# Down projections of a two-layer trunk: seven products of Strassen's scheme for eight, with the sums on GpSimd

## The chip, the cores and the metric

The kernel runs on one core of a Trainium2 chip. The metric is device time in microseconds (us) of one execution; three runs of the kernel before gave 1199.43, 1199.52 and 1201.88 us, median 1199.52. The granted TensorE clock of the profiled execution is 1.000.

## The reference

Two layers of a streaming encoder over 512 tokens of width 1024. Each layer mixes tokens (layer 0 with differential attention, layer 1 with chunked gated linear attention, both beside a cross-attention into 256 memory tokens) and then runs a gated feed-forward network with a causal depthwise convolution of width 3:

```python
def conv_ffn(h, w_up, conv_w, conv_b, w_down):
    u = h @ w_up                                  # 1024 -> 2 x 2816
    c = conv(u, conv_w) + conv_b                  # depthwise, causal, width 3
    a, g = jnp.split(c, 2, axis=-1)
    return (jax.nn.silu(g) * a) @ w_down          # 2816 -> 1024

for i in range(2):
    x = x + concat([mix, cross]) @ w_out[i]
    x = x + conv_ffn(rms_norm(x, ffn_norm[i]), w_up[i], conv_w[i], conv_b[i], w_down[i])
```

The change concerns the last product, `@ w_down`, in both layers: 2816 x 1024 weights against 512 tokens.

## The kernel before

Activations are held transposed, features on the 128 partitions and tokens along the columns: the residual stream is eight tiles `xT[n]` of [128 x 512]. Every large product runs in three TensorE passes on split numbers: a value is kept as a rounded high part (ScalarE copy, line 201 for weights) and the rest as a low part (VectorE subtraction, line 204), and `product` (lines 272 to 274) accumulates high x high, high x low and low x high. Weights come from one packed tensor in blocks of up to 1024 columns: a DMA into a `raw` buffer (three of them), then the split into `whi` and `wlo` (five of each). `weights(key)` hands out the pieces in the order of the list `_pieces` and has the next piece made ahead.

The feed-forward network (`ffn`, from line 1011) has 22 k tiles of 128 hidden features. For each, two up products of 24 matmuls (value half and gate half) go to one of the PSUM banks `ps_mm` and `ps_sm`; VectorE scales the bank into `u` (line 1026), ScalarE and VectorE run the convolution (1028 to 1030), ScalarE the Silu, VectorE the gating product (1057), and the result is split into a pair `mids` (1059 and 1060). After 12 k tiles, and again after the other 10 (`HALVES`), a down stage follows: for four blocks of 256 output features, two banks (`ps_lg`, `ps_tp`) take `product` over the tiles collected so far, each matmul with a [128 x 128] weight tile and 512 tokens, and `update` adds a finished bank to `xT[n]` (line 978). In the last down stage of layer 0 `update` also makes the next layer's operands: high part with the layer's gain (238), low part (239), square (338), running sum of squares (340). In the last stage of layer 1 each tile is sent out.

TensorE's order is as written in the code (a manual schedule over the whole kernel); the other engines are ordered by the scheduler, in the kernel before also beside the down stages. PSUM has eight banks, two for each of the tags `mm`, `sm`, `lg` and `tp`. Layer 1 begins with the projection `gm` of 272 columns (`gemm`, lines 255 to 257), whose first block needs all eight `xh`, `xl` tiles, followed by `token_rsqrt` (346).

Of the kernel before, what the change touches and what calls it, by code (L numbers as in the profile page):

```python
# [21 lines left out]
S = 512  # L22
# [8 lines left out]
HALVES = (6, 5)  # L31
XS = 36
WB = 5
STEPS, FILL = (8, 14, 20, 26), (3.2, 2.5, 1.2, 0.8, 1.3)
# [5 lines left out]
         [(c, (3, 4, 5)) for c in (0, 1, 2)] + [(3, (6, 7, 3, 4, 5))]])  # L40


def _pieces():
# [6 lines left out]
    for l in range(2):  # L50
# [29 lines left out]
def _blocks():  # L80

    out = []
    for key, name, i, ks, ranges in _pieces():
        w = sum(b - a for a, b in ranges)
        step = WTILE // w
        out.append([(name, i, ks[j:j + step], ranges, w) for j in range(0, len(ks), step)])
    return out
# [42 lines left out]
def trunk(ctx, tc, head_d, x_t, mem_t, wpack, cols_a_d, cols_d, conv_d, gate_d, rel_bias, diff_lambda, consts, onehot, out):  # L130
# [75 lines left out]
    def raw_tile():  # L206
        return wp.tile([128, WTILE], F32, name="raw", tag="raw", bufs=3)
# [5 lines left out]

    def make_piece(raws=None, between=None):
        parts = []
# [12 lines left out]
    def weights(key):  # L228
# [748 lines left out]
    def update(n, p, gain, acc):  # L977
        V.tensor_add(xT[n], xT[n], p)
        if gain is None:
            return  # L980
# [30 lines left out]
    def ffn(pool, l, acc):  # L1011
        rB = pool.tile([128, S], F32, name="rB", bufs=1)
        us = [pool.tile([128, S + 2], F32, name=f"u{i}", bufs=1) for i in range(4)]
# [4 lines left out]
        def up(parts, n):  # L1018
# [3 lines left out]
            product(p, parts, n, list(zip(xh, xl)))  # L1022
# [19 lines left out]
        base = 0  # L1042
        for half, nq in enumerate(HALVES):
            mids = []
            for q in range(base, base + nq):
                wa = weights(("ua", l, q))
                wg = None
                for n in range(2):
                    ua = up(wa, n)
                    wg = wg or weights(("ug", l, q))  # L1050
                    if q == 0 and n == 0:
                        row_scales(acc[0])
                    ug = up(wg, n)
                    ca = conv(*ua, 2 * q + n)
                    cg = conv(*ug, 22 + 2 * q + n)
# [112 lines left out]
```

## Time and profile before

| | |
|---|---|
| median of three runs | 1199.52 us |
| span of the profiled execution, first to last instruction | 1195.9 us |
| four down stages | 66.6, 55.6, 66.5 and 55.6 us |
| TensorE matmuls busy | 1178.8 us, 5656 instructions |
| VectorE busy | 761.1 us |
| ScalarE busy | 548.3 us |
| GpSimd busy | 4.5 us, 25 instructions |

The profiled execution's time is known as its span; the whole time that the runs state holds some 3.6 us more than it. In a row of the profile stand the line, the engine, the operation, the written and read tiles with their shapes and the count; then busy time and mean duration, and the idle time of the engine before these instructions with what ended it. PE is TensorE, PEld its weight loads, DVE VectorE, ACT ScalarE, POOL GpSimd, SP the engine that issues most DMAs. Durations of matmuls overlap; starts tell their rate.

### The profile page before, as it was taken

Reading aid. Unit: us, or ns where it says so; the run is one execution under the profiler, and the core shown is the slowest. Engines: PE = TensorE matmul, PEld = TensorE weight load, DVE = VectorE, ACT = ScalarE, POOL = GpSimd, SP = SyncE. Lnnn points to the kernel's source line nnn. Section 1 sums busy time; section 2 is a strip of 40 time slices with the busy share of each in tenths; the row PEclk is TensorE's granted clock in tenths of the full one; section 3 lists DMA queues with packets and bytes.
Section 4 is the critical chain, followed back from the end, with each engine's and each line's share of the span. In section 5 each row is a group of like instructions: output and inputs, shape, how many; then the busy total and the mean of one; then the engine's idle time right before and its main releaser. Section 6 shows DMA issues by size and latency. Waiting matters only on the chain.

```text
span 1195.9 us, 14770 instructions
## 1 busy us (share of the span) xinstructions
PE 1178.8 (99%) x5656; PEld 964.5 (81%) x5656; DVE 761.1 (64%) x1270; ACT 548.3 (46%) x966; POOL 4.5 (0%) x25
## 2 busy tenths in 40 slices
PE   9999998999999999999999999999999999999998
PEld 6887776788888888888888788988888888888887
DVE  7566676777777434767557736768777743476741
ACT  6666676554444322434436534536544422243420
POOL 0000000000000000000000000000000000000000
PEclk9999999999999999999999999999999999999999
DMA  8432213132332332422342221233233233232231
GB/s 296 124 96 80 80 54 119 50 120 92 106 106 71 123 100 63 123 85 89 115 129 93 72 71 58 89 104 125 84 106 105 74 121 106 70 123 72 89 115 44
DMA packets 39268, 117.81 MB, mean 99 GB/s; under 512 B 4671, under 2 KB 6520, under 8 KB 39198
## 3 DMA queue, kind: packets, MB, share of 16 engines
q1 hardware_dynamic: 39054, 116.62, 30.7%
q8 instruction: 44, 0.72, 0.2%
q14 instruction: 26, 0.21, 0.1%
q10 hardware_dynamic: 144, 0.26, 0.1%
HBM read 112.65 MB, written 4.21 MB: 98 GB/s over the span
## 4 chain that ended last, share of the span: by engine, by line
PE 90%; ACT 4%; DVE 3%; DMA 2%; issue 1%; SPq 0%; ACTq 0%; DVEq 0%
PE ps_mm L273 8%; PE ps_mm L274 8%; PE ps_mm L272 8%; PE ps_sm L273 7%; PE ps_sm L272 7%; PE ps_sm L274 7%; PE ps_mm L255 5%; PE ps_mm L257 5%; PE ps_mm L256 5%; PE ps_lg L273 3%; PE ps_lg L272 3%; PE ps_lg L274 3%; PE ps_tp L272 3%; PE ps_tp L273 3%; PE ps_tp L274 3%; PE ps_tp L170 2%
## 5 line engine op out<-in xcount | busy, mean ns | idle before, releaser
L201 ACT CAST whi<-raw 128x1024 fp32r<-128x1024 f32 (+4 forms) x212 | 208.4, 985 | 264.7 <-PE ps_tp L273 134.7
L204 DVE TENSOR_TENSOR wlo<-raw,whi 128x1024 fp32r<-128x1024 f32 (+4 forms) x212 | 241.3, 1140 | 113.3 <-ACT whi L201 110.9
L272 PE MATMUL ps_mm<-xsh,whi 128*128 128x512 f32 x438 | 173.3, 396 | 0.0
L273 PE MATMUL ps_mm<-xsl,whi 128*128 128x512 f32 x438 | 170.6, 390 | 0.2 <-DVE xsl L239 0.2
L274 PE MATMUL ps_mm<-xsh,wlo 128*128 128x512 f32 x438 | 170.6, 390 | 0.0
L272 PE MATMUL ps_sm<-xsh,whi 128*128 128x512 f32 x378 | 147.1, 389 | 0.0
L274 PE MATMUL ps_sm<-xsh,wlo 128*128 128x512 f32 x378 | 147.1, 389 | 0.0
L273 PE MATMUL ps_sm<-xsl,whi 128*128 128x512 f32 x378 | 147.0, 389 | 0.0
L255 PE MATMUL ps_mm<-whi,xsh 128*128 128x512 f32 (+2 forms) x352 | 136.7, 388 | 0.1
L257 PE MATMUL ps_mm<-whi,xsl 128*128 128x512 f32 (+2 forms) x352 | 131.1, 372 | 0.3 <-DVE xsl L239 0.3
L256 PE MATMUL ps_mm<-wlo,xsh 128*128 128x512 f32 (+2 forms) x352 | 130.6, 371 | 0.0
L1028 ACT ACTIVATE cvo<-u,cv 128x512 f32<-128x512 f32 x88 | 71.6, 814 | 121.5 <-DVE u L1026 121.5
L273 PEld LDWEIGHTS ps_mm<-xsl,whi 128*128 128x128 f32 x438 | 82.3, 188 | 17.4 <-DVE xsl L239 0.6
L274 PEld LDWEIGHTS ps_mm<-xsh,wlo 128*128 128x128 f32 x438 | 82.2, 188 | 17.2
L272 PEld LDWEIGHTS ps_mm<-xsh,whi 128*128 128x128 f32 x438 | 82.3, 188 | 17.1 <-issue 0.7
L1029 DVE SCALAR_TENSOR_TENSOR cvo<-u,cv,cvo 128x512 f32<-128x512 f32 x88 | 65.8, 749 | 38.7 <-ACT cvo L1028 38.7
L274 PEld LDWEIGHTS ps_sm<-xsh,wlo 128*128 128x128 f32 x378 | 70.9, 188 | 14.8
L272 PEld LDWEIGHTS ps_sm<-xsh,whi 128*128 128x128 f32 x378 | 71.0, 188 | 14.8
L273 PEld LDWEIGHTS ps_sm<-xsl,whi 128*128 128x128 f32 x378 | 71.0, 188 | 14.6
L255 PEld LDWEIGHTS ps_mm<-whi,xsh 128*128 128x128 f32 x352 | 66.3, 188 | 13.6 <-issue 3.3
L257 PEld LDWEIGHTS ps_mm<-whi,xsl 128*128 128x128 f32 x352 | 66.1, 188 | 12.5 <-DVE xsl L239 0.5
L256 PEld LDWEIGHTS ps_mm<-wlo,xsh 128*128 128x128 f32 x352 | 66.4, 189 | 9.8
(273 smaller groups left out, 1760.6 us busy)
## 6 DMA issues: line engine op xcount, KB each, us to landing
raw<-in_wpack_dram SPq DMA_DIRECT2D x178, 512.0 KB, 3.5
xt<-in_x_t_dram SPq DMA_DIRECT2D x15, 256.0 KB, 6.0
raw<-in_wpack_dram SPq DMA_DIRECT2D x15, 256.0 KB, 2.6
raw<-in_wpack_dram SPq DMA_DIRECT2D x8, 384.0 KB, 3.1
xres<-xt SPq DMA_DIRECT2D x8, 256.0 KB, 2.0
xt<-xres SPq DMA_DIRECT2D x8, 256.0 KB, 3.3
out_dram<-xt SPq DMA_DIRECT2D x8, 256.0 KB, 2.0
bt<-bias_d SPq DMA_DIRECT2D x6, 256.0 KB, 3.6
```

The lines of the kernel that those rows point to most:

```text
L170: nc.tensor.transpose(dst, src, ident[:n, :n])
L201: ins = A.copy(hi[:, c], raw[:, c])
L204: V.tensor_sub(lo[:, c], raw[:, c], hi[:, c].bitcast(F32))
L255: mm(p, sh[k][:, blk(b)], hi, start=k == 0, stop=False)
L256: mm(p, sh[k][:, blk(b)], lo, start=False, stop=False)
L257: mm(p, sl[k][:, blk(b)], hi, start=False, stop=k == KT - 1)
L272: mm(p, hi[:, blk(n)], bh, start=i == first, stop=False)
L273: mm(p, hi[:, blk(n)], bl, start=False, stop=False)
L274: mm(p, lo[:, blk(n)], bh, start=False, stop=i == last)
L1028: A.activation(c, u[:, 2:], AF.Identity, scale=cv[l][:, 2, j:j + 1], bias=cv[l][:, 3, j:j + 1])
L1029: V.scalar_tensor_tensor(c, u[:, 1:S + 1], cv[l][:, 1, j:j + 1], c, op0=ALU.mult, op1=ALU.add)
```

## The change

The down projection of a group of k tiles is cut in two along k (even and odd k tiles of a pair), along the output features (two blocks of 256 within each output half of 512) and along the tokens (two blocks of 256), and is computed with seven products of half size in each direction instead of eight (the variant of Strassen's scheme with 15 additions). The 22 k tiles make 11 pairs, in groups of 3, 4 and 4 pairs (`GROUPS`); after each group a down stage follows, and after the first two groups one further up tile is computed ahead of it. A stage has two output halves of seven products each, in the hand-written order of `DOWN`.

- Weights: per group and output half four quarters are loaded (`a11`, `a12`, `a22` and one that becomes `s3`), GpSimd makes the sums `s1` to `s4` from them, and seven blocks are split by ScalarE and VectorE, where four were. There are six `raw` buffers instead of three, and pieces are made further ahead (`prefetch`).
- Operands: per pair GpSimd makes four [128 x 256] differences (`middle`), and seven operands are split.
- Products: matmuls of a [128 x 128] weight tile with 256 tokens; some products accumulate onto a bank whose earlier state VectorE has already added.
- Additions: each product's state is added from PSUM to quarters of `xT` (`add`), 84 additions of 256 columns per layer.
- In the last group of a layer the first three products run over all pairs but the last one first.
- VectorE, ScalarE and GpSimd keep the written order in the down stages.
- The `us` buffers become slices of one tile at multiples of 544 columns. The scratch size for dynamic DMAs is set to 1024.

```diff
-HALVES = (6, 5)
+GROUPS = (3, 4, 4)
 XS = 36
 WB = 5
+RAWS = 6
+DOWN = ((0, "a11"), (0, "s1"), (0, "a12"), (0, "s2"), (0, "s4"), (0, "s3"), (1, "a11"), (0, "a22"),
+        (1, "s1"), (1, "s2"), (1, "a12"), (1, "s3"), (1, "s4"), (1, "a22"))
...
+def _ffn():
+
+    steps, q = [], 0
+    for i, nq in enumerate(GROUPS):
+        steps += [("up", t) for t in range(2 * q + (i > 0), 2 * (q + nq) + (i + 1 < len(GROUPS)))]
+        steps.append(("down", i))
+        q += nq
+    return steps
...
-        for nq in HALVES:
-            for q in range(base, base + nq):
-                piece(("ua", l, q), "w_up", l, K8, (256 * q, 256 * q + 256))
-                piece(("ug", l, q), "w_up", l, K8, (DFF + 256 * q, DFF + 256 * q + 256))
-            for c in range(4):
-                piece(("dn", l, base, c), "w_down", l, tuple(range(2 * base, 2 * base + 2 * nq)),
-                      (256 * c, 256 * c + 256))
-            base += nq
+        for what, i in _ffn():
+            if what == "up":
+                for h in range(2):
+                    f = DFF * h + 128 * i
+                    piece(("u", l, i, h), "w_up", l, K8, (f, f + 128))
+            else:
+                for c, name in DOWN:
+                    piece(("d", l, i, c, name), "w_down", l, (), (512 * c, 512 * c + 512))
...
+    wsums = {}
+
+    def make_sum(key, todo):
+        n, name = 256 * GROUPS[key[2]], key[4]
+        r = wsums.setdefault(key[:4], {})
+        v = lambda t: r[t][:, :n]
+        if name == "a11":
+            for t in ("a11", "s3", "a22", "a12"):
+                r[t] = load_raw(raw_tile(), n)
+            r["s1"], r["s2"] = raw_tile(), raw_tile()
+            G.tensor_add(v("s1"), v("s3"), v("a22"))
+            G.tensor_sub(v("s2"), v("s1"), v("a11"))
+            G.tensor_sub(v("s3"), v("a11"), v("s3"))
+        if name == "s4":
+            r["s4"] = r["a12"]
+            G.tensor_sub(v("s4"), v("s4"), v("s2"))
+        hi, lo = (wp.tile([128, WTILE], F32R, name=t, tag=t, bufs=WB) for t in ("whi", "wlo"))
+        split_weights(slice(0, n), r[name], hi, lo)
+        return hi, lo
+
     def make_piece(raws=None, between=None):
+        key = plan[len(made)][0]
+        if key[0] == "d":
+            made.append(make_sum(key, blocks[len(made)]))
+            return
...
+    def prefetch(i):
+        size = lambda j: 1 if plan[j][0][0] == "d" else len(blocks[j])
+        by_block = plan[i][0][0] in "ud"
+        while len(made) <= i or (len(made) < len(plan) and (
+                sum(map(size, range(i, len(made) + 1))) <= WB if by_block else len(made) < i + 2)):
+            make_piece()
+
+    def weights(key, more=True):
         i = used[0]
         assert plan[i][0] == key, (plan[i][0], key)
-        while len(made) < min(i + 2, len(plan)):
-            make_piece()
+        if more:
+            prefetch(i)
...
+        if gain is not None:
+            settle(n, gain, acc)
+
+    def settle(n, gain, acc):
         xh[n], xl[n] = split_tiles()
         split(xh[n], xl[n], xT[n], gain(n))
...
+        us = pool.tile([128, 4 * (S + 32)], F32, name="us", bufs=1)
+        us = [us[:, blk(i, S + 32)][:, :S + 2] for i in range(4)]
...
+        def middle(n, m, op, prev):
+            lo, hi = m[:, blk(0, 256)], m[:, blk(1, 256)]
+
+            def put(dst, src):
+                A.copy(dst[:, :, 0:256], src)
+                V.tensor_sub(dst[:, :, 256:512], src, dst[:, :, 0:256].bitcast(F32))
+            one = lambda t: t.rearrange("p (a b) -> p a b", a=1)
+            if n == 0:
+                t = pool.tile([128, 4, 256], F32, name="mt", bufs=1)
+                b11, t1 = (xs.tile([128, S], F32R, name=x, tag="xs", bufs=XS) for x in ("b11", "t1"))
+                G.tensor_sub(t[:, 0], hi, lo)
+                put(one(b11), one(lo))
+                put(one(t1), t[:, 0:1])
+                op.update(b11=b11, t1=t1)
+                return t, hi
+            t, hi0 = prev
+            G.tensor_sub(t[:, 1], hi, t[:, 0])
+            G.tensor_sub(t[:, 2], hi, hi0)
+            G.tensor_sub(t[:, 3], lo, t[:, 1])
+            r = pool.tile([128, 5, S], F32R, name="mid", bufs=max(GROUPS))
+            put(r[:, 0:2], m.rearrange("p (a b) -> p a b", a=2))
+            put(r[:, 2:5], t[:, 1:4])
+            op.update(zip(("b21", "b22", "t2", "t3", "t4"), (r[:, i] for i in range(5))))
+
+        def down(g, mids, finish):
+            last, ks = len(mids) - 1, tuple(range(len(mids)))
+            parts, banks, first = {}, {}, used[0]
+
+            def step(c, tag, w, m, ks=ks, start=False, more=True):
+                if (c, w) not in parts:
+                    parts[c, w] = weights(("d", l, g, c, w), more)
+                elif more:
+                    prefetch(first + more)
+                if start:
+                    banks[c, tag] = bank(tag)
+                p = banks[c, tag]
+                hi, lo = parts[c, w]
+                for k in ks:
+                    mv = mids[k][m]
+                    for n in range(2):
+                        o, ws = p[:, blk(n, 256)], slice(256 * k + 128 * n, 256 * k + 128 * n + 128)
+                        terms = (hi, mv[:, 0:256]), (hi, mv[:, 256:512]), (lo, mv[:, 0:256])
+                        for i, (a, b) in enumerate(terms):
+                            mm(o, a[:, ws], b, start=start and (k, n, i) == (0, 0, 0), stop=k == last and i == 2,
+                               skip_group_check=True)
+
+            def add(c, tag, f, t):
                 for n in range(2):
...
+                    x = xT[4 * c + 2 * f + n][:, blk(t, 256)]
+                    V.tensor_add(x, x, banks[c, tag][:, blk(n, 256)])
+
+            def done(c, f):
                 for n in range(2):
...
+                    finish(4 * c + 2 * f + n)
+            if g + 1 < len(GROUPS):
+                step(0, "lg", "a11", "b11", start=True)
+                add(0, "lg", 0, 0)
+                step(0, "tp", "s1", "t1", start=True)
+                add(0, "tp", 1, 1)
+                step(0, "mm", "a12", "b21", start=True)
+                add(0, "mm", 0, 0)
+            else:
+                step(0, "lg", "a11", "b11", ks[:-1], True)
+                step(0, "tp", "s1", "t1", ks[:-1], True, False)
+                step(0, "mm", "a12", "b21", ks[:-1], True, False)
+                step(0, "lg", "a11", "b11", ks[-1:], more=False)
+                add(0, "lg", 0, 0)
+                step(0, "tp", "s1", "t1", ks[-1:], more=1)
+                add(0, "tp", 1, 1)
+                step(0, "mm", "a12", "b21", ks[-1:], more=2)
+                add(0, "mm", 0, 0)
+            step(0, "lg", "s2", "t2")
+            add(0, "lg", 0, 1)
+            step(0, "tp", "s4", "b22")
+            add(0, "tp", 0, 1)
+            done(0, 0)
+            step(0, "lg", "s3", "t3")
+            add(0, "lg", 1, 1)
+            step(1, "lg", "a11", "b11", start=True)
+            add(1, "lg", 0, 0)
+            step(0, "lg", "a22", "t4")
+            add(0, "lg", 1, 0)
+            done(0, 1)
+            step(1, "tp", "s1", "t1", start=True)
+            add(1, "tp", 1, 1)
+            step(1, "lg", "s2", "t2")
+            add(1, "lg", 0, 1)
+            step(1, "mm", "a12", "b21", start=True)
+            add(1, "mm", 0, 0)
+            step(1, "lg", "s3", "t3")
+            add(1, "lg", 1, 1)
+            step(1, "tp", "s4", "b22")
+            add(1, "tp", 0, 1)
+            done(1, 0)
+            step(1, "lg", "a22", "t4")
+            add(1, "lg", 1, 0)
+            done(1, 1)
+
+        acc2, mids, live = [None], [], []
+
+        def finish(n):
+            if l == 0:
+                settle(n, lambda k: c_attn(1, k), acc2)
+                nc.sync.dma_start(xres[n], xT[n])
+            else:
+                nc.sync.dma_start(out[n], xT[n])
+        for what, i in _ffn():
+            if what == "up":
+                ua = up(weights(("u", l, i, 0)))
+                if i == 0:
+                    row_scales(acc[0])
+                ug = up(weights(("u", l, i, 1)))
+                ca = conv(*ua, i)
+                cg = conv(*ug, 22 + i)
+                A.activation(cg, cg, AF.Silu)
+                V.tensor_mul(ca, ca, cg)
+                if i % 2 == 0:
+                    live = [{}, None]
+                    mids.append(live[0])
+                live[1] = middle(i % 2, ca, *live)
+            else:
+                n, last = GROUPS[i], i == len(GROUPS) - 1
+                if last and l == 0:
+                    tables("natural_log_exp_and_others")
+                with tc.manual_schedule(engines={E.Activation, E.DVE, E.Pool}):
+                    down(i, mids[:n], finish if last else lambda n: None)
+                mids = mids[n:]
         return acc2
```

More of the change, by code (lines that the diff above doesn't have):

```diff
@@ L84, in _blocks @@
         w = sum(b - a for a, b in ranges)
+        if key[0] == "d":
+            base, (f, _) = sum(GROUPS[:key[2]]), ranges[0]
+            ks = [tuple(2 * q + j for q in range(base, base + GROUPS[key[2]])) for j in range(2)]
+            out.append([(name, i, ks[j], ((f + 256 * h, f + 256 * h + 256),), 256)
+                        for h, j in ((0, 0), (1, 0), (1, 1), (0, 1))] if key[4] == "a11" else [])
+            continue
         step = WTILE // w
@@ L206, in raw_tile @@
     def raw_tile():
-        return wp.tile([128, WTILE], F32, name="raw", tag="raw", bufs=3)
+        return wp.tile([128, WTILE], F32, name="raw", tag="raw", bufs=RAWS)
     def load_raw(raw, n):
@@ L1021, in up @@
             p = bank("mm" if i % 4 < 2 else "sm")
[L1022 removed]
+            product(p, parts, 0, list(zip(xh, xl)))
             return p, us[i % 4]
```

43 lines of the change are left out of this document (3 added, 40 removed).

## The prediction

> **What bounds the kernel now.** I read the page first, then the busy time by stage, then the timeline of TensorE and of VectorE where stages meet.
>
> ```profile
> span 1195.9 us, 14770 instructions
> PE 1178.8 (99%) x5656; PEld 964.5 (81%) x5656; DVE 761.1 (64%) x1270; ACT 548.3 (46%) x966; POOL 4.5 (0%) x25
> ...
> PEclk9999999999999999999999999999999999999999
> ...
> PE 90%; ACT 4%; DVE 3%; DMA 2%; issue 1%; SPq 0%; ACTq 0%; DVEq 0%
> ```
>
> TensorE is busy in 99% of the span at the full granted clock, and it makes 90% of the chain that ended last; GpSimd does next to nothing. So fewer TensorE microseconds are worth their whole length, as long as the other engines keep feeding it. Stage by stage (the four down stages, and one up stage):
>
> ```profile
> core 0: us, PE busy (x) PEld busy (x) DVE busy (x) ACT busy (x) POOL busy (x), PEclk, DMA share, GB/s
> ...
> 393.90:460.50 66.60, 66.60 (x290) 54.08 (x290) 23.12 (x25) 14.64 (x16) 0.00 (x0) 1.00 0.31 95
> 460.50:569.30 108.80, 108.80 (x481) 90.07 (x480) 76.31 (x96) 45.44 (x57) 0.00 (x0) 1.00 0.29 92
> 569.30:624.90 55.60, 55.59 (x241) 44.97 (x240) 27.59 (x37) 22.54 (x30) 1.67 (x4) 1.00 0.40 128
> ...
> 961.00:1027.50 66.50, 66.50 (x289) 54.02 (x288) 23.11 (x25) 14.57 (x15) 0.00 (x0) 1.00 0.30 95
> ...
> 1136.40:1192.00 55.60, 55.58 (x241) 44.77 (x239) 16.16 (x20) 9.09 (x11) 0.00 (x0) 1.00 0.24 80
> ```
>
> The down stages take 66.6 + 55.6 + 66.5 + 55.6 = 244.3 us for 2 x (288 + 240) = 1056 matmuls of 512 columns, 231 ns from one to the next; an up stage takes 108.8/480 = 227 ns. In a down stage VectorE works only 23.1 of 66.6 us, in an up stage already 76.3 of 108.8 (70%).
>
> **The products.** The change replaces 8 quarter products by 7, but halves the moving operand: 11 pairs of k tiles x 7 products x 2 output halves x 2 row blocks x 3 terms x 2 layers = 1848 matmuls of 256 columns, each with its own weight load. Does a 256-column matmul cost half? The listed durations overlap, so I read starts in the one place that has this shape in a row, 25 matmuls of the gated layer's last projection:
>
> ```profile
> start us, us, engine line op out<-in xcount [idle before <-releaser]
> 769.46 0.28 PE L257 MATMUL ps_mm<-whi,xsl 128*128 128x256 f32 x1
> ...
> 772.34 0.28 PE L257 MATMUL ps_mm<-whi,xsl 128*128 128x256 f32 x1
> ```
>
> (772.34 - 769.46)/24 = 120 ns, more than half of 227: some 13 ns per matmul don't shrink with the columns. New down time 1848 x 0.120 = 221.8 us, a gain of **22.5 us** (9% of the stage, not the eighth that seven for eight suggests). Bounds: half of 227 would give 209.8 (gain 34.5); if the new tiles cost 7 ns more, as the down stages' 231 against 227 warns at half width and beyond, 127 ns give 234.7 (gain 9.6). I take 120, since it is this very shape with a fresh weight load each time.
>
> **What the other engines must do for it.**
>
> ```profile
> L204 DVE TENSOR_TENSOR wlo<-raw,whi 128x1024 fp32r<-128x1024 f32 x178 | 217.3, 1223 | 92.7 <-ACT whi L201 91.6 <-PE ps_tp L170 0.2
> L201 ACT CAST whi<-raw 128x1024 fp32r<-128x1024 f32 x178 | 187.0, 1052 | 218.7 <-PE ps_tp L273 110.7 <-PE ps_sm L273 61.7 <-issue 25.2
> ...
> L338 ACT ACTIVATE xt<-xt 128x512 f32<-128x512 f32 x35 | 21.4, 621 | 0.0
> L340 DVE TENSOR_TENSOR xt<-xt 128x512 f32<-128x512 f32 x31 | 21.2, 684 | 0.2
> ...
> L978 DVE TENSOR_TENSOR xt<-xt,ps_lg 128x512 f32<-128x512 f32 x16 | 11.0, 688 | 68.4 <-PE ps_lg L274 68.4
> ...
> L204 DVE TENSOR_TENSOR wlo<-raw,whi 128x768 fp32r<-128x768 f32 x8 | 7.6, 956 | 4.6 <-ACT whi L201 3.3 <-DMA xt<-in_x_t_dram 1.3
> ...
> L201 ACT CAST whi<-raw 128x768 fp32r<-128x768 f32 x8 | 6.6, 836 | 9.9 <-PE ps_mm L273 6.3 <-PE ps_mm L257 3.6
> ...
> L204 DVE TENSOR_TENSOR wlo<-raw,whi 128x256 fp32r<-128x256 f32 x8 | 3.4, 420 | 3.9 <-ACT whi L201 3.9
> ...
> L239 DVE SCALAR_TENSOR_TENSOR xsl<-xt,cols_a,xsh 128x512 fp32r<-128x512 f32 x8 | 6.0, 748 | 3.2 <-ACT xsh L238 3.2
> L238 ACT ACTIVATE xsh<-xt,cols_a 128x512 fp32r<-128x512 f32 x8 | 5.8, 726 | 18.2 <-DVE xt L978 18.2
> ...
> L828 POOL MEMSET xt<- 128x512 f32 x1 | 0.5, 530 | 51.8 <-PE ps_tp L170 51.8
> ...
> L435 POOL MEMSET gw<- 96x384 f32 x1 | 0.4, 414 | 0.0
> ...
> raw<-in_wpack_dram SPq DMA_DIRECT2D x178, 512.0 KB, 3.5
> ```
>
> Weight splits in the down stages grow from 22 to 38.5 blocks of 1024 columns per layer (seven summed quarters for four): +16.5 x 1.22 = 20 us on VectorE and 17 on ScalarE. Adds from PSUM go from 16 of 512 columns (11 us) to 84 of 256 at 0.42 (35 us), operand splits from 22 x 0.69 = 15 to 11 x 2.5 = 27 us. That is some 57 us more per layer on VectorE, 64% to about 74% of the span: no new bound. In a group of four pairs one product is 24 x 0.120 = 2.88 us of TensorE, and VectorE has per product one split and two adds, 1.22 + 0.84 = 2.06; in a group of three, 2.16 against 0.96 + 0.84 = 1.80. It keeps up, with little over. The order is written out by hand there: the split for the product four ahead stands in front of this product's adds, and an accumulation into a used bank waits for the add before it. Behind every late sum or split stand adds, and behind these TensorE, with about one product of slack.
>
> The weight loads are as many bytes as before. The reuse of the six raw buffers lets the second half's third tile (3.5 us) land before the first product starts; only the second and later sums of that half wait, for the split of the quarter a22. That is four to five products ahead of use, so I cost the loads at nothing.
>
> GpSimd sums are not in the trace. From below a [128 x 1024] sum can hardly beat VectorE's 1.22 us; from above, three passes (two reads, one write) at the memset's slope, (530 - 414)/128 = 0.9 ns a column, make 2.8 us. I take 2.0, between them: 33 blocks' worth per layer, 66 us beside some 340 us of feed-forward network. [...]
>
> **Where TensorE will wait nonetheless.** First, the last group of each layer, where nothing covers the chain behind the last up product:
>
> ```profile
> 569.50 0.69 DVE L1026 TENSOR_TENSOR u<-ps_sm,rB 128x512 f32<-128x512 f32 x1 [0.59 <-PE ps_sm L274]
> ...
> 573.78 0.69 DVE L1057 TENSOR_TENSOR cvo<-cvo 128x512 f32<-128x512 f32 x1 [0.70 <-ACT cvo L1056]
> ```
>
> The gated product is ready at 574.5, 5.2 us after the last up matmul (569.3). Then come three dependent GpSimd subtractions (some 0.5 us each), a 768-column copy (0.84) and its subtraction (0.96): 8.7 us with the hops, and only behind that VectorE adds the first product (0.84). TensorE has three products to do meanwhile, 8.64 us, and then needs that add: about 1.2 us late, 2.4 in both layers. Second, in layer 0's last group the operands of layer 1 are made between the adds (per tile a scaled copy of 0.73, a square of 0.62 and two VectorE steps). Behind the fifth product's add, which ends 1.0 us after its product, ScalarE has two such tiles, 2.7, and the next split's copy, 1.05; then VectorE has that split's 1.22 and the sixth product's add, 0.84. That is 6.8 us where two products, 5.76, are covered: 1.0 late, the same again behind the eighth product, and I add 1.0 for the shift of the first point: 3 us. Third, the layer boundary:
>
> ```profile
> 624.94 0.29 PE L255 MATMUL ps_mm<-whi,xsh 128*128 128x272 f32 x1
> ...
> 628.30 0.39 PE L257 MATMUL ps_mm<-whi,xsl 128*128 128x272 f32 x1 [0.31 <-DVE xsl L239]
> 628.90 1.05 PE L346 MATMUL ps_sm<-C,xt 128*128 128x1 f32 x8 [0.21 <-DVE xt L340]
> 629.81 0.38 PE L255 MATMUL ps_mm<-whi,xsh 128*128 128x272 f32 x1
> ```
>
> The first 24 matmuls of layer 1 take 4.9 us before, some 1.7 more than fed ones. Now both last tiles get their last add only after the last product. VectorE is then still some 3 us behind with the pair before (adds, two splits, two tiles); the adds take 0.84, and copy, square, copy and low part of the two tiles 0.73 + 0.62 + 0.73 + 0.75 = 2.8: the last operand comes about 7 us after the last product, where the fed matmuls cover 3. Some 4.4 us lost for 1.7: 3 us more than before. Fourth, VectorE's convolutions beside the groups of three: 1 us each, 2. Fifth, two 256-column adds instead of one of 512 at the end: 0.2. Together 10.6 us.
>
> Sixth, GpSimd against VectorE. No row of before shows a two-input sum on GpSimd beside VectorE. From below nothing; from above VectorE stands still during the sums (rival below). I take 2.4 us, 0.4 per group, half a collision of one sum less the slack. [...]
>
> Sum: -22.5 + 10.6 + 2.4 = -9.5. The span is 1195.9 and the median 1199.52, 3.6 us around it, which I leave as they are: **1190.0 us**.
>
> **Rivals.**
> (a) *All fed.* If the queue orders hide the waits, 1199.5 - 22.5 = 1177. For it: VectorE's 2.06 in 2.88. Against it: the chain of 8.7 us is there. Chance 0.15.
> (b) *The shared port decides: slower.* In each group the second half's sums s2, s3, s4 stand back to back on GpSimd, 3 x 2.0 = 6.0 us. If VectorE's splits can't run beside them, the add of the sixth product is 6.0 late against a slack of 2.88 - 1.0 = 1.9: 4.1 us in each of six groups, 24.6. 1199.5 - 22.5 + 10.6 + 24.6 = 1212. [...] It decides from (22.5 - 10.6)/6 = 2.0 us per group. Chance 0.22. About that point, within 0.2% (2.4 us, about what a measurement here can tell from no change): 0.08.
> (c) *Narrow matmuls are dearer.* At 127 ns: 1199.5 - 9.6 + 13 = 1203. Only 13 ns carry over per matmul in the row of this shape. Chance 0.05.
> (d) *It doesn't do what it says.* The built program has 1848 matmuls of 256 columns and 1056 fewer of 512: excluded.
>
> **How the numbers follow.** Forecast (1184 to 1196) 0.50, (a) 0.15, in between 0.08, (b) 0.22, (c) 0.05. Faster: 0.50 + 0.15 + 0.01 = 0.66; same 0.06; slower 0.28. The range reaches from (a) to just short of (b)'s price, 1178 to 1210; its own range as the likeliest case is 1184 to 1196.
>
> **What would show it.** Down stages with 256-column starts 120 ns apart and 222 us plus their waits; waits of TensorE on VectorE's adds from PSUM, above all in layer 0's last group; GpSimd some 130 us in all. The forecast is wrong if VectorE's 1024-column split, 1.22 us before, is much longer beside GpSimd (b), or starts lie above 125 ns (c).

## The result: slower by 3%

The changed kernel takes 1234.62 us (median of four runs, 1233.69 to 1237.44) against 1199.47 us for the kernel before in the same comparison: a ratio of 1.0299 with a 95% interval of 1.028 to 1.0317. The forecast of 1190.0 us had the sign wrong and the time lies above its range. Rival (b), splits of VectorE that wait beside GpSimd's sums, came true (the split's mean went from 1223 to 1354 ns); its price, 24.6 us, was about half of what it cost, 51.2 us.

From the profile's page of the changed kernel: its span, its engines and the granted clock in 40 slices:

```profile
span 1231.9 us, 16978 instructions
PE 1175.7 (95%) x6448; PEld 1003.1 (81%) x6448; DVE 929.3 (75%) x1486; ACT 601.6 (49%) x1046; POOL 220.1 (18%) x161
PEclk9999999999999999999898999999999999999989
```

TensorE is busy in 95% of the span instead of 99%. VectorE has gone from 761.1 to 929.3 us, GpSimd from 4.5 to 220.1 (the prediction said some 130), and the clock line shows three slices below 9 where it had none. The busy time by stage, for the six down stages:

```profile
core 0: us, PE busy (x) PEld busy (x) DVE busy (x) ACT busy (x) POOL busy (x), PEclk, DMA share, GB/s
339.70:377.20 37.50, 32.26 (x255) 31.88 (x254) 33.35 (x50) 16.55 (x21) 9.88 (x6) 0.95 0.43 136
464.20:511.90 47.70, 42.54 (x338) 41.98 (x338) 41.13 (x53) 19.53 (x22) 16.19 (x8) 0.96 0.39 122
588.00:642.50 54.50, 44.59 (x337) 43.35 (x337) 45.24 (x62) 26.87 (x35) 15.45 (x13) 0.91 0.34 105
928.70:965.60 36.90, 32.43 (x253) 31.86 (x253) 33.33 (x50) 16.55 (x21) 9.84 (x6) 0.95 0.44 139
1052.60:1100.30 47.70, 42.37 (x338) 41.81 (x337) 41.17 (x53) 19.53 (x22) 16.20 (x8) 0.96 0.39 122
1176.40:1228.00 51.60, 43.89 (x338) 42.68 (x336) 37.41 (x51) 16.18 (x19) 13.83 (x9) 0.90 0.15 52
```

The windows are rounded outwards a little; from the first down matmul to the end of the last the six stages take 275.1 us, where 1848 matmuls at 120 ns would take 221.8. So 53.3 us are waiting or slow clock, and the stages lost 30.9 us against the 244.2 of before. VectorE is busy for 41.13 of 47.70 us in the second stage, where the plan gave it 2.06 us of every 2.88 (72%). What TensorE (PE) waits for most in the down stages, over the whole kernel, as line and tile waiting, releaser, total, times, longest:

```profile
PE ps_lg L1138 <- DVE xt L1144: 26.4, 15, 3.5
PE ps_mm L1138 <- ACT mid L1099: 8.1, 2, 4.1
PE ps_lg L1138 <- ACT cvo L1209: 2.6, 1, 2.6
```

L1138 is the down matmul, L1144 the add from PSUM, L1099 the copy of an operand's high part, L1209 the Silu. The adds are not slow themselves. The groups of instructions of the changed kernel say which are (the first row is from the kernel before, its second convolution step):

```profile
L1030 DVE SCALAR_TENSOR_TENSOR cvo<-u,cv,cvo 128x512 f32<-128x512 f32 x88 | 66.1, 751 | 2.9
...
L223 DVE TENSOR_TENSOR wlo<-raw,whi 128x1024 fp32r<-128x1024 f32 x194 | 262.3, 1354 | 33.6 <-ACT whi L220 32.5 <-PE ps_tp L189 0.2
L1083 DVE SCALAR_TENSOR_TENSOR cvo<-us,cv,cvo 128x512 f32<-128x512 f32 x88 | 92.1, 1047 | 2.9
L1144 DVE TENSOR_TENSOR xt<-xt,ps_lg 128x256 f32<-128x256 f32 x96 | 35.9, 412 | 12.4 <-PE ps_lg L1138 12.4
L245 POOL TENSOR_TENSOR raw<-raw 128x1024 f32<-128x1024 f32 x8 | 24.5, 3062 | 0.3
L244 POOL TENSOR_TENSOR raw<-raw 128x1024 f32<-128x1024 f32 x8 | 20.0, 2506 | 17.1 <-issue 11.7 <-DVE wlo L223 5.5
L1113 POOL TENSOR_TENSOR mt<-cvo,mt 128x256 f32<-128x256 f32 x22 | 34.7, 1576 | 0.0
L1111 POOL TENSOR_TENSOR mt<-cvo,mt 128x256 f32<-128x256 f32 x22 | 16.2, 736 | 216.0 <-DVE cvo L1210 216.0
```

The split (L223) has a mean of 1354 ns instead of 1223, the second convolution step (L1083) 1047 instead of 751; both read two SBUF tiles. The add that reads PSUM and SBUF (L1144) takes 412 ns, as forecast from 420. On GpSimd the same subtraction of 256 columns takes 736 ns in one place (L1111) and 1576 in another (L1113). How one wait comes about is seen in the timeline of GpSimd, VectorE, ScalarE and TensorE ahead of the second down stage (start, duration, engine, instruction, idle time before it and its releaser):

```profile
459.92 2.78 POOL L248 TENSOR_TENSOR raw<-raw 128x1024 f32<-128x1024 f32 x1 [5.97 <-DVE wlo L223]
460.48 2.77 DVE L1083 SCALAR_TENSOR_TENSOR cvo<-us,cv,cvo 128x512 f32<-128x512 f32 x1
...
466.59 1.21 DVE L223 TENSOR_TENSOR wlo<-raw,whi 128x1024 fp32r<-128x1024 f32 x1
466.64 1.76 POOL L1113 TENSOR_TENSOR mt<-cvo,mt 128x256 f32<-128x256 f32 x1
468.43 0.83 ACT L1099 CAST mid<-mt 128x768 fp32r<-128x768 f32 x1 [2.19 <-POOL mt L1113]
469.30 0.96 DVE L1100 TENSOR_TENSOR mid<-mt,mid 128x768 fp32r<-128x768 f32 x1 [1.50 <-ACT mid L1099]
...
474.81 0.75 DVE L1144 TENSOR_TENSOR xt<-xt,ps_lg 128x256 f32<-128x256 f32 x2
475.70 0.47 PE L1138 MATMUL ps_lg<-mid,whi 128*128 128x256 f32 x2 [2.66 <-DVE xt L1144]
```

The convolution step at 460.48 starts 0.56 us after a GpSimd sum has started and ends 0.55 us after the sum's end (463.25 and 462.70): it is 2.0 us late. Then the roles change: the subtraction at 466.64 starts just behind VectorE's split and ends at 468.40, 0.6 us after the split's end at 467.80, so GpSimd has lost 1.0. ScalarE's copy and VectorE's next step wait for that (1.50 us of VectorE idle in its written order), the adds at 474.81 stand behind, and TensorE has waited 2.66 us when it gets its bank. The two delays, 2.0 and 1.0, together are longer than that wait; that delays of this kind cause the waits is what the experiments below test.

The rest of the 36.0 us by which the span grew lies mostly at the layer boundary. Between the last down stage of layer 0 and the first of layer 1 the kernel before had 336.1 us with 12 k tiles; the changed one has 7 there. The five up tiles moved away are 5 x 10.88 us (108.8 for ten, above), so 281.7 would be equal, and it took 286.2: 4.5 us more. The end after the last product takes 4.3 us for 3.9.

### The profile page after: what moved, and what is told of

Read it like the earlier page. It is cut to its first block, busy times and chain, and to the rows that moved or that the text cites. A ratio compares the mean times of both kernels' runs of the same rounds, so it can differ in the third digit from the quotient of the medians.

```text
span 1231.9 us, 16978 instructions
## 1 busy us (share of the span) xinstructions
PE 1175.7 (95%) x6448; PEld 1003.1 (81%) x6448; DVE 929.3 (75%) x1486; ACT 601.6 (49%) x1046; POOL 220.1 (18%) x161
## 5 line engine op out<-in xcount | busy, mean ns | idle before, releaser
L223 DVE TENSOR_TENSOR wlo<-raw,whi 128x1024 fp32r<-128x1024 f32 (+3 forms) x248 | 313.7, 1267 | 42.3 <-ACT whi L220 41.1
L220 ACT CAST whi<-raw 128x1024 fp32r<-128x1024 f32 (+3 forms) x248 | 241.3, 980 | 182.0 <-PE ps_lg L1138 39.3
L1138 PE MATMUL ps_lg<-mid,whi 128*128 128x256 f32 x528 | 106.4, 302 | 29.0 <-DVE xt L1144 26.4
L1138 PEld LDWEIGHTS ps_lg<-mid,whi 128*128 128x128 f32 x528 | 89.4, 208 | 32.1 <-issue 18.1
L1081 ACT ACTIVATE cvo<-us,cv 128x512 f32<-128x512 f32 x88 | 71.7, 815 | 52.2 <-DVE us L1079 51.5
L1083 DVE SCALAR_TENSOR_TENSOR cvo<-us,cv,cvo 128x512 f32<-128x512 f32 x88 | 92.1, 1047 | 2.9
```

What stands on the lines that cost most here:

```text
L220: ins = A.copy(hi[:, c], raw[:, c])
L223: V.tensor_sub(lo[:, c], raw[:, c], hi[:, c].bitcast(F32))
L1081: A.activation(c, u[:, 2:], AF.Identity, scale=cv[l][:, 2, j:j + 1], bias=cv[l][:, 3, j:j + 1])
L1083: V.scalar_tensor_tensor(c, u[:, 0:S], cv[l][:, 0, j:j + 1], c, op0=ALU.mult, op1=ALU.add)
L1138: mm(o, a[:, ws], b, start=start and (k, n, i) == (0, 0, 0), stop=k == last and i == 2, skip_group_check=True)
```

## The experiments

The theory that this suggests: VectorE's instructions with two SBUF operands and GpSimd's sums exclude each other. Shared port is the prediction's and the expectations' name for this; what the runs show is which instructions hold each other up and for how long, not a port. Rivals: VectorE simply has too much to do; GpSimd's sums are too slow and come too late, whatever VectorE does.

**All sums on VectorE.** Every sum and difference leaves GpSimd, each weight sum is formed just ahead of its use:

```diff
-            G.tensor_add(v("s1"), v("s3"), v("a22"))
+            V.tensor_add(v("s1"), v("s3"), v("a22"))
...
-                G.tensor_sub(t[:, 0], hi, lo)
+                V.tensor_sub(t[:, 0], hi, lo)
```

> All sums of weights and operands move from GpSimd to VectorE (each summed quarter is formed just ahead of the splits that need it); results stay the same. Shared-port theory: the VectorE rows go back to the durations they have alone (L1083-type convolution step 1047 ns to about 750, 1024-column split 1354 to about 1220), VectorE takes some 45 us more per layer, the waits of TensorE in the down stages fall from 54 us to 15 to 25, and the time is 1195 to 1205 us. Load theory (VectorE has too much to do in the down stages, GpSimd is harmless): more work on VectorE makes it worse than 1234.6 us. Latency theory (TensorE waits for the slow GpSimd sums themselves): about 1210 us, because a sum takes half the time on VectorE.

Measured: 1194.54 us, ratio to the kernel before 0.9963 (0.9951 to 0.9976). The page's engines, the split and the waits:

```profile
span 1188.9 us, 16894 instructions
PE 1162.5 (98%) x6448; PEld 992.1 (83%) x6448; DVE 926.4 (78%) x1622; ACT 600.9 (51%) x1046; POOL 4.6 (0%) x25
L223 DVE TENSOR_TENSOR wlo<-raw,whi 128x1024 fp32r<-128x1024 f32 x194 | 236.5, 1221 | 36.4 <-ACT whi L220 34.7 <-PE ps_tp L189 0.2
PE ps_lg L1141 <- DVE xt L1147: 7.3, 7, 3.0
```

VectorE is busy for as long as in the changed kernel (926.4 and 929.3 us), now with work in place of waiting, and the kernel is 40 us faster; the split is back at 1221 ns. Too much work on VectorE is refuted. The down stages take 231.4 us, 9.6 more than fed ones, so both the waits and the time came out a little below what the shared-port theory expected (15 to 25 us, and 1195 to 1205).

**GpSimd that only writes.** The sums stay on GpSimd in their places, but each works on 2 columns, and the rest is filled with a constant, twice, so this kernel leaves the sums out:

```diff
+    def g_sum(op, o, a, b, w):
+        op(o[:, 0:2], a[:, 0:2], b[:, 0:2])
+        G.memset(o[:, 2:w], 0.5)
+        G.memset(o[:, 2:w], 0.5)
```

> GpSimd keeps its place and its waits, but reads next to nothing: each sum is made on 2 columns only, and the other columns are written twice with a constant (the sums are thus left out). A 1024-column sum then holds GpSimd for about 2.0 us instead of 2.5. Shared-port theory, with reads as the point of contention: VectorE durations as without GpSimd (750 and 1220 ns), waits of TensorE in the down stages under 20 us, 1192 to 1200 us. Theory that any GpSimd access, writes too, stops VectorE: durations stay long, 1220 to 1234 us. Load or latency theory: within 10 us of 1234, since order, waits and nearly the length of the sums stay.

Measured: 1181.99 us in one execution, below even the 1192 to 1200 expected if reads are the point. Its second down stage in the view by stage:

```profile
457.10:497.40 40.30, 40.30 (x337) 40.26 (x336) 30.05 (x46) 16.64 (x18) 10.17 (x13) 1.00 0.42 142
```

TensorE is busy for the whole stage, 7.4 us shorter than the 47.70 of the changed kernel. Then the same with three fills, so that GpSimd is at least as slow as in the changed kernel:

> As the run in which GpSimd only writes (each sum on 2 columns, the rest left out and filled instead), with three fills for two, so that a block of 1024 columns keeps GpSimd for about 0.4 + 3 x 0.95 = 3.2 us and one of 256 for 1.3: longer than the sums of the changed kernel (2.5 to 3.06 and 0.74 to 1.58), with GpSimd busy for 240 us or more. If the waits came from sums that are late, and not from the port, the down stages wait at least as long as in the changed kernel, 53 us, and the time is above 1230. If the port alone does it, the splits stay at 1.22, the waits below 8 us, and the time at 1182 to 1190.

Measured: 1182.54 us in one execution. The page, GpSimd's fills of 1022 columns and VectorE's split in this second kernel:

```profile
PE 1160.8 (98%) x6448; PEld 992.2 (84%) x6448; DVE 856.3 (73%) x1486; ACT 601.4 (51%) x1046; POOL 233.1 (20%) x569
L239 POOL MEMSET raw<- 128x1022 f32 x32 | 30.5, 954 | 1.7
L223 DVE TENSOR_TENSOR wlo<-raw,whi 128x1024 fp32r<-128x1024 f32 x194 | 236.7, 1222 | 43.9 <-ACT whi L220 42.3 <-PE ps_tp L189 0.2
```

GpSimd is busy for longer than in the changed kernel (233.1 against 220.1 us), yet the down stages take 223.2 us for 221.8 fed, and the time is 52 us below. This is what the port theory expected (1182 to 1190). That the sums come too late of themselves is refuted; the cost goes with GpSimd's reading of its operands (1234.62 us with the sums, 1182.54 with the fills).

**One kind of sum at a time.** First the weight sums on VectorE with the operand differences on GpSimd, then the other way round:

> Only the weight sums move to VectorE; the operand differences of [128 x 256] stay on GpSimd. Shared-port theory: the long collisions (2.5 us each) go, the short ones (0.7 to 1.2 us) stay, mostly in the up stages; waits of TensorE in the down stages 20 to 30 us, 1203 to 1212 us. Load theory: worse than 1234 us. Latency theory: between 1205 and 1220 us.

> Only the operand differences move to VectorE; the weight sums stay on GpSimd. Shared-port theory: the stalls in the middle of each down stage stay (some 7 us per group), only the chain at the start of the last groups gets shorter by 2 to 3 us in each layer: 1226 to 1231 us. Latency theory of the operand chain: the 4 us waits of TensorE at the start of the last groups fall below 1 us, 1224 us. Load theory: slower than 1236 us.

Measured, in one execution each: 1204.68 us with only the operand differences on GpSimd, 1217.04 with only the weight sums there. Over the 1194.54 of all sums on VectorE that is 10.1 us for the differences and 22.5 for the weight sums; both together cost 40.1, that is 7.5 more than their sum. The executions of one kernel lie up to 6 us apart here, so from single ones these shares are rough. The first result is within the 1203 to 1212 us expected of the shared port; the second is below all that was expected (1224 at the least), so the differences in the changed kernel cost more than the expectation gave them.

**Extra sums in the kernel before.** The contention without Strassen's product: for each of the 48 blocks of down weights GpSimd makes one sum that nobody reads, behind ScalarE's copy, when VectorE's split becomes ready too.

```diff
             split_weights(slice(0, n * w), raw, hi, lo, len(made) == 2)
+            if plan[len(made)][0][0] == "dn":
+                G.tensor_add(extra[0][:, :n * w], raw[:, :n * w], hi[:, :n * w].bitcast(F32))
```

> The kernel before, with one extra GpSimd sum of two SBUF operands for each block of the down weights (raw + whi into a tile that nobody reads), so that it starts when VectorE's split of the same block does. If VectorE and GpSimd exclude each other for whole instructions when both read two SBUF operands, those splits last 1.22 + up to 2.5 us (1024 columns: 2.5 to 3.8 in the records), while adds from PSUM stay at 0.69 us; the time hardly moves (within 5 us), since VectorE has slack in these down stages. If the cost is spread in small slices (each slowed by half), the splits last about 1.8. If the trouble in the changed kernel is of its own making, they stay at 1.22.

Measured: 1230.83 us in one execution, 31 us more than before; the expectation of "within 5 us" was far off, the one on the splits was met (it gave the sums of the changed kernel as 2.5 to 3.8 us; its trace has 2.37 to 3.41). VectorE and GpSimd at the end of an up stage, and what TensorE waited for:

```profile
393.49 0.68 DVE L1029 TENSOR_TENSOR u<-ps_sm,rB 128x512 f32<-128x512 f32 x1
394.09 2.84 DVE L204 TENSOR_TENSOR wlo<-raw,whi 128x1024 fp32r<-128x1024 f32 x1
396.85 2.89 DVE L1063 TENSOR_TENSOR midl<-cvo,midh 128x512 fp32r<-128x512 f32 x1
399.66 2.89 DVE L1032 SCALAR_TENSOR_TENSOR cvo<-u,cv,cvo 128x512 f32<-128x512 f32 x1
...
389.53 6.31 POOL L224 TENSOR_TENSOR extra<-raw,whi 128x1024 f32<-128x1024 f32 x2 [10.19 <-ACT whi L201]
396.15 5.85 POOL L224 TENSOR_TENSOR extra<-raw,whi 128x1024 f32<-128x1024 f32 x2 [0.31 <-POOL extra L224]
PE ps_lg L274 <- ACT midh L1062: 21.0, 4, 5.5
```

While four sums follow each other on GpSimd, VectorE gets one instruction in per sum, each ending 2.81 us after the one before it, whether it would take 1.22 (L204), 0.69 (L1063) or 0.75 us alone (L1032). The product with a PSUM operand (L1029) takes its usual 0.68 us beside them. The last operands of the down stage come late for it: 21.0 us of TensorE in four waits. Beside these waits stand four stretches at half clock, 23.9 us together (the granted clock is 0.989 over the span), which can account for the rest of the 31 us. The slack of VectorE in the down stages, on which the expectation relied, did not count: the sums collided at the end of the up stage, where the chain to the next operands has none.

**Extra copies in the kernel before.** The same, with a copy of one operand for the sum:

```diff
+                G.tensor_copy(extra[0][:, :n * w], hi[:, :n * w].bitcast(F32))
```

> The kernel before with the same 48 extra GpSimd instructions as the run with extra sums, but each a copy of one SBUF operand (whi) instead of a sum of two. If any GpSimd read of SBUF keeps a two-operand VectorE instruction out until it ends, the splits beside a copy again reach 2.8 us or the copy's length plus 1.2, and the time is above 1215. If only GpSimd's two-operand instructions take the port, no VectorE instruction is longer than 1.25 us and the time stays at 1199 to 1201.

Measured: 1200.08 us in one execution. GpSimd's copy and VectorE's split:

```profile
389.74 1.05 POOL L224 COPY extra<-whi 128x1024 f32<-128x1024 f32 x1 [0.73 <-ACT whi L201]
390.07 1.78 DVE L204 TENSOR_TENSOR wlo<-raw,whi 128x1024 fp32r<-128x1024 f32 x1
L224 POOL COPY extra<-whi 128x1024 f32<-128x1024 f32 x40 | 73.4, 1835 | 587.8 <-ACT whi L201 587.6
L204 DVE TENSOR_TENSOR wlo<-raw,whi 128x1024 fp32r<-128x1024 f32 x178 | 223.2, 1255 | 91.4 <-ACT whi L201 90.3 <-PE ps_tp L170 0.2
```

Neither expectation holds whole. A GpSimd read of one operand did keep a two-operand VectorE instruction out: the split at 390.07 ends 1.06 us after the copy, nearly a whole split later, and the longest took 2.06 us. The copies are held up too: 1.05 us for this one, 1.84 in the mean. But that is still less than a sum of the changed kernel, 2.37 us at the least, and the time did not move.

**Sums in quarters.** The changed kernel with each weight sum cut into pieces of 256 columns:

```diff
+    def g_sum(op, o, a, b, n):
+        for j in range(0, n, 256):
+            op(o[:, j:j + 256], a[:, j:j + 256], b[:, j:j + 256])
```

> The changed kernel with each weight sum of 1024 columns cut into four GpSimd instructions of 256 columns (768: three), the same columns in all. If VectorE waits for a whole GpSimd instruction and then gets its turn, no VectorE instruction waits longer than one quarter (0.7 to 0.9 us): the longest splits fall from 3.03 to about 2.0 us, the waits of TensorE in the down stages from 53 to 25 to 40 us, the time to 1205 to 1222. If VectorE gets the port only when GpSimd's queue of sums is empty, the splits stay at 3 us and longer and the time at 1230 or above. If the sum of both engines' port time alone counts, the time stays within 5 us of 1234.6.

Measured: 1235.24 us in one execution; on the time the third expectation held. The longest split fell to 1.80 us, as the first had it, but neither the waits of TensorE nor the time followed. The page's engines, VectorE's split, and a quarter of a weight sum:

```profile
PE 1179.8 (96%) x6448; PEld 1008.2 (82%) x6448; DVE 883.4 (72%) x1486; ACT 601.5 (49%) x1046; POOL 270.1 (22%) x289
L223 DVE TENSOR_TENSOR wlo<-raw,whi 128x1024 fp32r<-128x1024 f32 x194 | 241.9, 1249 | 48.2 <-ACT whi L220 47.1 <-PE ps_tp L189 0.2
L237 POOL TENSOR_TENSOR raw<-raw 128x256 f32<-128x256 f32 x176 | 177.4, 1040 | 136.1 <-DVE wlo L223 111.8 <-issue 18.4 <-DMA raw<-in_wpack_dram 6.0
```

VectorE is held up less (883.4 us busy for 929.3, the split 1249 ns for 1354), but now GpSimd is the one that waits: a quarter takes 1040 ns where the undisturbed subtraction of 256 columns (L1111 of the changed kernel) takes 736, so that a whole sum of 1024 columns takes 4.2 us instead of 2.5 to 3.1, and everything behind a sum comes later. The down stages take 273.8 us, hardly less than the 275.1 of the whole sums. Cutting the sums shorter only moved the wait from one engine to the other. That what counts is the time for which both engines read SBUF fits this, but it was not tested on its own. The run also shows that the fills of the runs before were not harmless for being short: these quarters are about as short (1040 ns, the fills 954), and they cost as much as whole sums (1235.24 us against 1234.62).

**The remaining waits of the version on VectorE.** First s3 is formed behind the split of s2, then, besides, layer 1's first weights are split before the last tiles of layer 0 and not between them.

```diff
-            V.tensor_sub(v("s3"), v("a11"), v("s3"))
+        if name == "s2":
+            V.tensor_sub(v("s3"), v("a11"), v("s3"))
```

> The kernel with all sums on VectorE, with one edit: the weight sum s3 is formed behind the split of s2 instead of right behind s2, so that VectorE never has two 1024-column sums and a split in a row. If the 5.3 us of waits left in layer 0's last group come from such a pile of VectorE work ahead of an add, they fall to about 3 us and the span falls by 2 us (about 1192.5). If they come from the operands of layer 1 (ScalarE's copies and squares between the adds), they stay at 5 and the time stays at 1194.5.

```diff
-            split_weights(slice(0, n * w), raw, hi, lo, len(made) == 2)
+            split_weights(slice(0, n * w), raw, hi, lo, len(made) == 2 or plan[len(made)][0] == ("g", 0))
...
-                got.extend(weights(key))
+                got.extend(weights(key, key[0] != "gm"))
...
             V.tensor_scalar_mul(rh[:, :NB], r, 0.5)
+            while len(made) <= used[0]:
+                make_piece()
```

> As the run with s3 spread, and besides the first weights of layer 1's gated projection are split before the last tiles of layer 0 instead of between them (two splits of 1.22 us and two copies of 1.05 us leave that place). If these splits hold up the last operands, the stretch between the last down stage of layer 0 and the first of layer 1 falls from 286.7 to about 282 us, the half clock of 6.8 us there goes with its wait, and the time is 1187 to 1189. If the last adds and operands alone set it (as the prediction had it), it stays at 285 to 287 and the time is within 1 us of the run with s3 spread.

Measured: 1193.89 us with s3 moved (ratio to the kernel before 0.9943, 0.9927 to 0.996), 1192.53 with both (0.9941, 0.992 to 0.9962). The waits of layer 0's last group were 6.8 us in the first and 5.3 in the second, no less than the 5.3 of the version before them, so that pile is not their cause; and the stretch at the boundary fell only from 286.7 to 285.9, though TensorE's longest wait there went from 1.89 to 0.40 us. The half clock of 6.8 us there did not go with that wait, as had been expected: from 627.97 to 634.80 us the granted clock is 0.50, and matmuls of 272 columns start 227 ns apart instead of 125; by that some 3 us go there, an estimate. Both expectations of a gain failed. The last version is the fastest that computes everything, but its interval overlaps with those of its neighbours.

**One line of the change in the kernel before.** The change also makes the u tiles slices of one tile. That line alone:

```diff
-        us = [pool.tile([128, S + 2], F32, name=f"u{i}", bufs=1) for i in range(4)]
+        us = pool.tile([128, 4 * (S + 32)], F32, name="us", bufs=1)
+        us = [us[:, blk(i, S + 32)][:, :S + 2] for i in range(4)]
```

> The kernel before with one line of the change alone: the four u tiles become slices of one tile, 32 columns of padding each, which moves every later tile of the feed-forward pool by a multiple of 128 bytes. In the kernel before the down matmuls start 231 ns apart and the up matmuls 227. If that is where the tiles named mid lie, the starts become 227 in the down stages and the time falls by 1056 x 4 ns = 4 us, to 1195; then part of the change's gain is this line and not Strassen's product. If it has to do with the down stages themselves, the time stays at 1199.3.

Measured: 1196.01 us, ratio 0.9967 (0.9953 to 0.9981). Two of its down stages in the view by stage:

```profile
395.60:460.90 65.30, 65.30 (x290) 54.08 (x289) 23.10 (x25) 14.64 (x16) 0.00 (x0) 1.00 0.30 97
569.70:624.40 54.70, 54.60 (x241) 44.91 (x240) 27.49 (x37) 22.56 (x30) 1.68 (x4) 1.00 0.40 130
```

65.3/288 = 227 ns where 66.6 us made 231. So the 231 in the kernel before went with the placement of its tiles, which is all that this line changes, and the four down stages lose 4.2 us of their 244.2 by this line alone.

## Why the prediction was wrong, step by step

**The products: right.** In the second down stage of the kernel whose GpSimd only writes, 336 matmuls take 40.3 us, 120 ns each, and all six stages take 223.1. The 22.5 us were there. But 4.2 of them belong to the line on the u tiles; against the kernel before with that line, Strassen's product is worth 240.0 - 221.8 = 18.2. The prediction read the 231 against 227 as a warning about half width (its bound of 127 ns); it was a matter of placement.

**The waits of the written order: 10.6 forecast, about 6 there.** They are read from the kernel with three fills, whose GpSimd is as slow as in the changed one. First, the last group's chain: 2.4 forecast, nothing in layer 1 (in layer 0 it can't be told from the second). Second, the operands of layer 1: 3 forecast, 1.5. Third, the layer boundary: 3 forecast, 4.0 (285.7 for 281.7), and 4.7 with two fills; TensorE does wait 1.9 us for the last operands there, but 3.4 us of the stretch (6.8 with two fills) ran at half clock, which the prediction did not have. Fourth, groups of three: 2 forecast, 0. Fifth, the end: 0.2 forecast, 0.4. "It keeps up, with little over" was right about VectorE's work, in this kernel.

**A GpSimd sum: too low.** 2.0 us was taken between 1.22 and 2.8; the sums took 2.37 us at the least and 2.5 to 3.06 in the mean, and the whole of GpSimd 220 us for 130. For the path this matters only through the next step.

**GpSimd against VectorE: the step that failed.** The sixth term took 2.4 us, "half a collision of one sum less the slack", 0.4 per group. Measured, as the changed kernel's span over that of the one with three fills: 1231.9 - 1180.7 = 51.2 us, twenty times as much. The prediction let a collision be soaked up by the slack of about one product. In the runs a VectorE instruction that meets a sum lasts until shortly after the sum ends (2.77 us for 0.75, to 0.55 us after the sum), GpSimd is held up in its turn (1.76 us for 0.74), and behind both stand the adds that TensorE waits for. The runs tell two kinds of GpSimd work apart: beside a sum, which reads two SBUF tiles, a step of 0.75 us took 2.77; beside fills, which only write, that step's mean is 751 ns and the split's 1222, for 751 and 1223 in the kernel before. No run shows the 0.4 per group: it was an estimate of the author's, and the runs showed 8.5 in its place.

**Rival (b): right in kind, half in size.** It priced the second half's weight sums alone, at 24.6 us. In the runs weight sums on GpSimd cost 22.5 us more than on VectorE, and the kernel that has only them there is 34.5 us (1217.04 - 1182.54) above the one whose GpSimd only writes; part of that is VectorE's work on the operand differences. Nor do the second half's sums all stand back to back: in the second down stage s2 and s3 start at 484.03 and 486.37 us, s4 at 492.78. It left out the rest. It counted only the splits as VectorE's party, where convolution steps, gating products and the operands' low parts are of the same kind (L1083 went from 751 to 1047 ns). It left out the operand differences on GpSimd, 10.1 us above the same on VectorE. It let only VectorE wait, while GpSimd waits as well (L1113 at 1576 for 736 ns), which lengthens the chain to the operands. And it did not know the clock, below. Against its own decision point, 2.0 us per group, the 51.2 us are 8.5 per group.

**What would show it: right.** TensorE's largest waits are on VectorE's adds from PSUM, as forecast, but for another reason. The prediction named the split beside GpSimd as the sign of (b), and 1354 ns for 1223 is that sign; for a mean over 194 instructions it looks small, because most of them meet no sum, and those that do meet one take up to 3.03 us.

**What is left open.** In the last version of the experiments the down stages take 11 us more than fed ones, and the boundary some 4. In the kernel with three fills the down stages take only 1.4 more, so most of the 11 came with the sums on VectorE; which of them hold up the adds is open, as moving s3 did not help. Of the 4 at the boundary about 3 are half clock; why the clock falls there without a longer wait than 0.40 us is open too.

**The 3.6 us around the span: a slip without effect.** Where a run's time and span are both on record they lie 1.8 us apart, in the changed kernel (1233.69 and 1231.9) and in the kernel before (1197.73 and 1195.9). The 3.6 us compare a median with another execution's span; the forecast only takes 9.5 us off the median, so nothing hangs on it.

## What to carry to other kernels

In these runs GpSimd was no free third engine for sums beside a VectorE that subtracts SBUF tiles: the convolution step took 1047 ns in the mean for 751. Adding up such instructions of both engines was no safe budget: in the second down stage those of VectorE take about 20 us (in the kernel with three fills) and GpSimd's sums at their shortest about 13, together 33 of the 40.3 us that TensorE needs, or 43 with the rest of VectorE's work, and the stage took 47.7. Look in the order of each engine for the instruction that a sum will meet, and for what stands behind it. Cutting the instructions shorter did not help here; moving the sums to VectorE did (40 us), where a sum takes 1.22 us instead of 2.37 or more and meets no other. And look at what else rides along in a change: the placement of four tiles was worth 4.2 us, about as much as Strassen's product brought at its best with the sums on VectorE (1192.53 against 1196.01 us, with overlapping intervals).

## What the runs showed of the hardware

The granted clock fell to 0.50 during and after short waits of TensorE. The changed kernel around its longest one, in the view by stage:

```profile
587.90:599.40 11.50, 8.23 (x68) 7.99 (x66) 9.37 (x13) 5.59 (x8) 0.85 (x2) 1.00 0.28 90
599.40:609.60 10.20, 6.85 (x28) 6.26 (x29) 6.61 (x9) 5.67 (x6) 4.92 (x4) 0.50 0.00 1
609.60:615.00 5.40, 5.40 (x46) 5.34 (x45) 5.40 (x7) 1.05 (x1) 2.86 (x2) 0.99 0.01 3
```

Waits of 4.08 and 2.36 us (ending at 600.21 and 604.77) stand with 10.2 us at a clock of 0.50. Before its end, the changed kernel has seven such stretches of 3.4, 6.8 or 10.2 us, and some 100 of its 256-column matmuls start about 213 ns apart instead of 120: about 9 of the 53 us. In the version with all sums on VectorE a wait of 1.89 us at the layer boundary goes with 6.8 us at half clock. Four of the changed kernel's seven stretches stand beside waits of only 1.77 to 2.66 us; the waits at the other three are 3.47, 4.06 and 4.08 us. The length of one wait did not decide it: in the version with all sums on VectorE a wait of 3.02 us (ending at 600.68) has no half clock beside it, and at the boundary of the last version 6.8 us of it follow waits of 0.40 us at most. Waits of TensorE were thus dearer here than their own length, by the 9 us above in the changed kernel, and the prediction, like its rival (b), priced them at their length.
